# Three chunked recurrences recast from chunks of 64 tokens to blocks of 128

## The chip, the cores and the metric

The kernel runs on one core of one Trainium2 chip. The metric is the device time of one execution in microseconds (us), from the profiler's clock; lower is better. The core has a matrix engine (TensorE, in the profile PE, with its weight loads as PEld), a vector engine (VectorE, DVE), a scalar engine (ScalarE, ACT), GpSimd (POOL) and a queue that issues DMAs (SyncE, SP). The profile also shows the clock that was granted to TensorE as a share of its full level.

## The reference, cut to what matters

Two models of two layers each run one after the other on the same 256 tokens of width 1024. Three recurrences in them are computed chunk by chunk; the reference's chunk is 64 tokens, but each recurrence has the same value for any chunk length.

```python
# 1. HGRN2, in both layers of the first model: 4 heads, dk = dv = 128, log_f per channel
cum = cumsum(log_f)                       # inside a chunk
a   = tril((q*exp(cum-ref)) @ (k*exp(ref-cum)).T)
o   = a @ v + (q*exp(cum)) @ state
state = exp(last)*state + (k*exp(last-cum)).T @ v

# 2. GLA, in the first layer of the second model: 4 heads, dk = 64, dv = 128, the same form,
#    in two directions, over a context of 256 tokens (state only) and then over the 256 tokens

# 3. gated delta rule (GDN), beside GLA: 4 heads, dk = dv = 128, one log decay per token and head
decay = exp(gc_t - gc_s) for s <= t
lmat  = strict_tril((k*beta) @ k.T * decay) + I
u     = lmat^-1 (beta*v - beta*exp(gc)*(k @ state))
o     = exp(gc)*(q @ state) + (q @ k.T * decay) @ u
state = exp(last)*state + (k*exp(last-gc)).T @ u
```

The rest is projections, attention, gated feed-forward layers and, in the last layer, a long convolution through Fourier matrices whose filters are made by a small network.

## The kernel before, in words

Nearly all of TensorE's work are the projections. Each weight is loaded by SP (L470), rounded to a high part by ScalarE (L471), its remainder taken by VectorE (L472), and three products of 128 by 128 weights with 256 tokens are accumulated (L485 to L487, or L521 to L523 where the tokens are the stationary side). A plain float32 product, as the recurrences use, is two instructions in the trace: the 16 calls of L947 are x32 there. The order of instructions on every engine is laid down at build time by a planner that simulates the program; it lets independent work of later lines move forward into waits.

The recurrences stand at these places:

- `br_c_pair` (L892), the HGRN2 of two heads, four times in all (two layers, two pairs). Sums of the log gates inside a chunk (L947, L969), scores by `chunk_scores` (L1081: two products, L1085 and L1087, so that the masked corner is never computed), `masked` (L1090), three state updates (L988 to L995), and the outputs (L1004, L1007).
- `ctx_gla` and `ctx_gdn` run GLA and GDN over the context, next to the feed-forward parts of the first model, so that their small steps lie between projections. `b2_layer0` runs both over the tokens.
- `gla_gates` (L1303) makes the gates and, over the tokens, the scores; `gla_scan` (L1390) walks through four chunks in each direction (L1417, L1419, L1433).
- `gdn` (L1501): gates (L1581 to L1617), decay matrices G (L1619 to L1641), the products with keys and queries (L1657 to L1677), the inverses, and the scan. `block_inverses` (L1461) makes inverses of 16 by 16 blocks on VectorE; L1691 to L1717 double them to 32 and to 64 (L1708 and L1714 on TensorE, a copy between them on ScalarE, a masked copy behind them on VectorE). The scan (L1739 to L1786) takes four chunks in each direction: keys times state (L1749), the right side (L1755), the inverse (L1760), its copy (L1761), the new state (L1765, L1771), queries times state (L1776). L1797 adds the part inside the chunks.

A chunk of 64 tokens takes 64 of the 128 partitions, so its products fill half of the array's rows or columns, or a quarter of the array; in the trace such forms are written 64\*64, 64\*128 or 128\*64 (weight rows by weight columns). In the scans the four heads of a step follow one another in the same half.

`filters` (L2005) makes the filters of the long convolution in eight rounds: loads of a window, a skip row and weights, L2033 and L2044 on TensorE, one addition of the skip row on GpSimd (L2038), and two tiles (fs, fd) written to memory (L2054). It is called for behind the scans of `b2_layer0`, and the planner has moved it into them.

Of the kernel before, what the change touches and what calls it, by code (L numbers as in the profile page):

```python
# [44 lines left out]
def _constants():  # L45
# [17 lines left out]
    add("rev0", same & (i[:, None] > i[None, :]))  # L63
    add("rev1", same & (i[:, None] < i[None, :]))
    j = np.arange(64)
    add("cm0", lo[:, None] <= j[None, :])
    add("cm1", lo[:, None] >= j[None, :])
# [25 lines left out]
def _constants2():  # L93
    f = np.float32
    i = np.arange(128)
    lo = i % 64
    j = np.arange(64)
    parts = []

    def add(name, a):  # L100
        a = np.asarray(a, f).reshape(128, -1)
        o = sum(p.shape[1] for p in parts)
        CST2_COLS[name] = (o, a.shape[1])
        parts.append(a)

    add("neg0", np.where(lo[:, None] <= j[None, :], 0.0, NEG))
    add("neg1", np.where(lo[:, None] >= j[None, :], 0.0, NEG))
# [3 lines left out]
    add("upper", np.stack([i // 32 % 2 == 0, i // 32 % 2 == 1], 1))  # L111
# [139 lines left out]
class K:  # L251
# [640 lines left out]
    def br_c_pair(self, l, p, hh, hl, lp, bh, bl, first):  # L892
# [47 lines left out]

        e1 = lp.tile([128, 2, S], F32, name="ce1")
        e2 = lp.tile([128, 2, S], F32, name="ce2")
        e3 = lp.tile([128, 2, S], F32, name="ce3")
        ps = self.aux()
        for h in range(2):
            for tb in range(2):
                nc.tensor.matmul(ps[:, h * S + tb * 128:h * S + (tb + 1) * 128], lf[:, tb, h * 128:(h + 1) * 128],  # L947
                                 self.c("tri0"), start=True, stop=True)
        v = ps.rearrange("p (c t) -> p c t", t=64)
        ref = lp.tile([128, 8, 1], F32, name="cref")  # L950
# [3 lines left out]
        nc.scalar.activation(e3, ps.rearrange(M2, m=2), AF.Exp)  # L954
        nc.scalar.activation(e2, e1, AF.Exp, scale=-1.0)
        nc.scalar.activation(e1, e1, AF.Exp)
        nc.vector.scalar_tensor_tensor(e1, e1, 0.5, hq, op0=OP.mult, op1=OP.mult)
        dl = lp.tile([128, 2, 4], F32, name="cdl")
        nc.vector.tensor_copy(dl, e3.rearrange("p h (c t) -> p h c t", t=64)[:, :, :, 63])
        nc.vector.scalar_tensor_tensor(e3, e3, 0.5, hq, op0=OP.mult, op1=OP.mult)  # L960
# [5 lines left out]
        nc.vector.tensor_tensor(e2, e2, ps.rearrange(M2, m=2), OP.mult)  # L966
        ps = self.aux()
        for tb in range(2):
            nc.tensor.matmul(ps[:, tb * 256:(tb + 1) * 256], self.c("rev0"), lf[:, tb, :], start=True, stop=True)  # L969
        nc.scalar.activation(e, ps.rearrange(M2, m=2), AF.Exp)  # L970
        nc.vector.tensor_tensor(hk, hk, e, OP.mult)

        AT = lp.tile([128, 4, 64], F32, name="cAT")
        nc.vector.memset(AT, 0.0)
        ps = self.aux()
        for h in range(2):
            for c in range(4):
                u, tb = c % 2, c // 2
                o = (tb * 2 + h) * 64
# [3 lines left out]
        ST = lp.tile([128, 3, 2, 128], F32, name="cST")  # L983
        for c in range(3):
            u, tb = c % 2, c // 2
            ps = self.aux()
            for h in range(2):
                nc.tensor.matmul(ps[:, h * 128:(h + 1) * 128], hk[64 * u:64 * u + 64, tb, h * 128:(h + 1) * 128],  # L988
                                 hv[64 * u:64 * u + 64, tb, h * 128:(h + 1) * 128], start=True, stop=True)
            if c == 0:  # L990
                nc.vector.tensor_copy(ST[:, 0, :, :], ps[:, :256].rearrange("p (h v) -> p h v", h=2))
            else:
                for h in range(2):
                    nc.vector.scalar_tensor_tensor(ST[:, c, h, :], ST[:, c - 1, h, :], dl[:, h, c:c + 1],
                                                   ps[:, h * 128:(h + 1) * 128], op0=OP.mult, op1=OP.add)  # L995
        on = lp.tile([128, 2, 256], F32, tag="cz", name="con")
        ss = lp.tile([128, 4], F32, name="css")
        for tb in range(2):
            po = self.aux()
            for h in range(2):  # L1000
                for u in range(2):
                    c = 2 * tb + u
                    o = po[64 * u:64 * u + 64, h * 128:(h + 1) * 128]
                    nc.tensor.matmul(o, AT[64 * u:64 * u + 64, tb * 2 + h, :],  # L1004
                                     hv[64 * u:64 * u + 64, tb, h * 128:(h + 1) * 128], start=True, stop=(c == 0))
                    if c:
                        nc.tensor.matmul(o, e3[:, h, c * 64:(c + 1) * 64], ST[:, c - 1, h, :], start=False, stop=True)  # L1007
# [73 lines left out]
    def chunk_scores(self, ps, o, u, k, q, d):  # L1081

        nc = self.nc
        full, part = (32, 0) if d == 0 else (0, 32)
        nc.tensor.matmul(ps[64 * u:64 * u + 64, o + full:o + full + 32], k, q[:, full:full + 32], start=True, stop=True)  # L1085
        p = 64 * u + part
        nc.tensor.matmul(ps[p:p + 32, o + part:o + part + 32], k[:, part:part + 32], q[:, part:part + 32], start=True,  # L1087
                         stop=True)

    def masked(self, dst, ps, d):  # L1090

        nc = self.nc
        n = dst.shape[1]
        m = self.c(f"cm{d}").bitcast(U32)
        full, part = (32, 0) if d == 0 else (0, 32)
        nc.vector.copy_predicated(dst[:, :, full:full + 32], m[:, None, full:full + 32].to_broadcast([128, n, 32]),
                                  ps[:, :, full:full + 32])
        for u in range(2):
            r = slice(64 * u + part, 64 * u + part + 32)
            nc.vector.copy_predicated(dst[r, :, part:part + 32], m[r, None, part:part + 32].to_broadcast([32, n, 32]),  # L1100
                                      ps[r, :, part:part + 32])
# [201 lines left out]
    def gla_gates(self, qT, kT, v, lat, smallT, lp, lt):  # L1303
# [16 lines left out]
        q3s, ATs, kds, dls = [], [], [], []  # L1320
        for d in range(2):
# [14 lines left out]
            dl = lp.tile([128, 2, 4], F32, name=f"ldl{d}")  # L1336
            dls.append(dl)
            if lat:
                ps = self.aux()
                for p in range(2):  # L1340
                    for b in range(2):
                        nc.tensor.matmul(ps[:, p * S + b * 128:p * S + (b + 1) * 128],
                                         la[:, b, p * 128:(p + 1) * 128], self.c(f"tri{d}"), start=True, stop=True)
                cv = ps.rearrange(V2, t=64)
                ri = 32 if d == 0 else 31
# [3 lines left out]
                e2 = lt.tile([128, 2, S], F32, tag="le2", name="le2")  # L1349
                e3 = lp.tile([128, 2, S], F32, name=f"le3{d}")  # L1350
                nc.vector.tensor_tensor(e1.rearrange("p a (c t) -> p (a c) t", t=64), cv,
                                        ref.to_broadcast([128, 8, 64]), OP.subtract)
                nc.scalar.activation(e3, ps.rearrange(M2, m=2), AF.Exp, scale=R)
                nc.scalar.activation(e2, e1, AF.Exp, scale=-R)
                nc.scalar.activation(e1, e1, AF.Exp, scale=R)
                nc.vector.tensor_tensor(e1, e1, qT, OP.mult)
                nc.vector.tensor_tensor(e2, e2, kT, OP.mult)
                li = 63 if d == 0 else 0
                nc.vector.tensor_copy(dl, e3.rearrange("p a (c t) -> p a c t", t=64)[:, :, :, li])
                nc.vector.tensor_tensor(e3, e3, qT, OP.mult)  # L1360
                q3s.append(e3)
                AT = lp.tile([128, 8, 64], F32, name=f"lAT{d}")
                nc.vector.memset(AT, 0.0)
                for r in range(2):
                    pa = self.aux()
                    for p in range(2):
                        for c in range(4):
                            u, b = c % 2, c // 2
                            o = (p * 2 + b) * 64
                            self.chunk_scores(pa, o, u, e2[64 * r:64 * r + 64, p, c * 64:(c + 1) * 64],  # L1370
                                              e1[64 * r:64 * r + 64, p, c * 64:(c + 1) * 64], d)
                    self.masked(AT[:, r * 4:r * 4 + 4, :], pa[:, :256].rearrange(V2, t=64), d)
                ATs.append(AT)
            else:
                ps = self.aux()
                for p in range(2):
                    for b in range(2):
                        nc.tensor.matmul(ps[:, p * 4 + b * 2:p * 4 + b * 2 + 2], la[:, b, p * 128:(p + 1) * 128],
                                         self.c("ind64"), start=True, stop=True)
                nc.scalar.activation(dl.rearrange("p a c -> p (a c)"), ps[:, :8], AF.Exp, scale=R)  # L1380
# [865 lines left out]
```

## Time and profile before

| | before |
|---|---|
| time, median of 3 runs | 2060.65 us (2053.74 to 2062.47) |
| the profiled execution | 2056.23 us, span 2054.2 us |
| TensorE busy | 2017.5 us, 98% |
| VectorE, ScalarE, GpSimd busy | 1506.2, 1034.1, 86.1 us |
| mean granted clock of TensorE | 0.982 of full |
| HBM read | 366.27 MB |

Busy time of TensorE counts an instruction from its start to the end of its passage through the array, and instructions overlap there. What an instruction costs the engine is therefore read from the distance between starts: a projection product of 256 columns is 0.28 us long in the timeline, but the next starts 0.12 us later.

### The profile page before, as it was taken

What the parts mean: (1) busy time and instruction counts of PE and PEld (TensorE: products, weight loads), DVE (VectorE), ACT (ScalarE), POOL (GpSimd) and SP (SyncE); (2) the same over time, 40 slices, a digit from 0 to 9 for tenths busy, and PEclk for the clock granted to TensorE, in tenths of its full rate; (3) what the DMA queues carried; (4) which work ended last, traced back from release to release, by engine and by line L of the source; (5) the groups of instructions that cost most, each with busy time, mean ns of one, the idle gap of its engine ahead of it and who ended that gap; (6) DMA issues with size and microseconds to landing.
All of it is one profiled execution on the core that took longest, in us unless ns stands there. A gap on an engine that the chain in (4) does not pass through costs nothing.

```text
span 2054.2 us, 40596 instructions
## 1 busy us (share of the span) xinstructions
PE 2017.5 (98%) x16666; PEld 1918.1 (93%) x16666; DVE 1506.2 (73%) x2491; ACT 1034.1 (50%) x1604; POOL 86.1 (4%) x80
## 2 busy tenths in 40 slices
PE   8999999999999999999999999999989999999998
PEld 8999999999999899999999989897779999899998
DVE  6968877896876868977777855885667555997554
ACT  6553455575544654454655434662135445756443
POOL 0000000010000000000000001000010000001001
PEclk9999999999999999999999999997999999999999
DMA  9854655975567755747654534452215667445664
GB/s 327 274 180 154 222 195 173 320 253 184 188 223 241 236 164 176 244 146 263 203 162 145 175 113 146 161 160 80 68 40 176 195 187 234 156 133 176 194 187 132
DMA packets 118562, 379.36 MB, mean 185 GB/s; under 512 B 18239, under 2 KB 28776, under 8 KB 117096
## 3 DMA queue, kind: packets, MB, share of 16 engines
q1 hardware_dynamic: 118376, 376.76, 56.3%
q8 instruction: 131, 2.15, 0.4%
q14 instruction: 55, 0.45, 0.1%
HBM read 366.27 MB, written 10.25 MB: 183 GB/s over the span
## 4 chain that ended last, share of the span: by engine, by line
PE 92%; DVE 2%; ACT 2%; issue 2%; DMA 1%; POOL 0%; SPq 0%; DVEq 0%; POOLq 0%; ACTq 0%
PE mm L487 22%; PE mm L485 22%; PE mm L486 22%; PE mm L522 1%; PE mm L521 1%; PE mm L523 1%; PE aux L1235 1%; ACT wh L471 1%; DVE wl L472 1%; PE aux L1760 1%; PE aux L1085 1%; PE aux L1765 1%; PE aux L2096 1%; PE mm L2044 1%; PE aux L2079 1%
## 5 line engine op out<-in xcount | busy, mean ns | idle before, releaser
L471 ACT CAST wh<-w 128x1024 fp32r<-128x1024 f32 (+2 forms) x570 | 589.0, 1035 | 665.5 <-PE mm L486 513.1
L472 DVE TENSOR_TENSOR wl<-w,wh 128x1024 fp32r<-128x1024 f32 (+2 forms) x570 | 685.3, 1203 | 290.9 <-ACT wh L471 288.6
L485 PE MATMUL mm<-hh,wh 128*128 128x256 f32 (+1 forms) x1776 | 503.5, 284 | 1.3 <-ACT wh L471 0.7
L487 PE MATMUL mm<-hh,wl 128*128 128x256 f32 (+1 forms) x1776 | 502.0, 283 | 1.1 <-DVE wl L472 1.1
L486 PE MATMUL mm<-hl,wh 128*128 128x256 f32 (+1 forms) x1776 | 502.1, 283 | 0.0
L485 PEld LDWEIGHTS mm<-hh,wh 128*128 128x128 f32 (+1 forms) x1776 | 335.7, 189 | 6.0 <-issue 3.6
L487 PEld LDWEIGHTS mm<-hh,wl 128*128 128x128 f32 (+1 forms) x1776 | 335.7, 189 | 5.1 <-issue 3.0
L486 PEld LDWEIGHTS mm<-hl,wh 128*128 128x128 f32 (+1 forms) x1776 | 335.9, 189 | 3.9 <-issue 2.6
L485 PE MATMUL mm<-xh,wh 128*128 128x256 f32 x960 | 268.7, 281 | 1.0 <-ACT uc L422 0.9
L487 PE MATMUL mm<-xh,wl 128*128 128x256 f32 x960 | 267.5, 279 | 1.6 <-DVE wl L472 1.5
L486 PE MATMUL mm<-xl,wh 128*128 128x256 f32 x960 | 268.3, 281 | 0.2
L487 PE MATMUL mm<-ph,wl 128*128 128x256 f32 x704 | 197.0, 280 | 0.0
L485 PE MATMUL mm<-ph,wh 128*128 128x256 f32 x704 | 196.8, 280 | 0.0
L486 PE MATMUL mm<-pl,wh 128*128 128x256 f32 x704 | 196.6, 279 | 0.0
L487 PEld LDWEIGHTS mm<-xh,wl 128*128 128x128 f32 x960 | 180.3, 188 | 5.2 <-issue 2.5
L485 PEld LDWEIGHTS mm<-xh,wh 128*128 128x128 f32 x960 | 180.4, 188 | 4.1 <-issue 2.2
L486 PEld LDWEIGHTS mm<-xl,wh 128*128 128x128 f32 x960 | 179.8, 188 | 3.8 <-issue 3.0
L1229 DVE SCALAR_TENSOR_TENSOR macc<-mw,cs,macc 128x512 f32<-128x512 f32 x196 | 145.7, 748 | 11.6 <-DMA mw<-in_t_mod_w 10.8
L487 PEld LDWEIGHTS mm<-ph,wl 128*128 128x128 f32 x704 | 132.1, 188 | 1.9 <-issue 1.9
L486 PEld LDWEIGHTS mm<-pl,wh 128*128 128x128 f32 x704 | 132.3, 188 | 1.5 <-issue 1.4
L485 PEld LDWEIGHTS mm<-ph,wh 128*128 128x128 f32 x704 | 132.2, 188 | 1.6 <-issue 1.5
L487 PE MATMUL mm<-brh,wl 128*128 128x256 f32 x384 | 107.5, 281 | 0.0
(679 smaller groups left out, 3595.3 us busy)
## 6 DMA issues: line engine op xcount, KB each, us to landing
w<-in_t_w_in SPq DMA_DIRECT2D x148, 512.0 KB, 4.2
w<-in_t_ffn_w SPq DMA_DIRECT2D x128, 512.0 KB, 4.3
mw<-in_t_mod_w SPq DMA_DIRECT2D x96, 512.0 KB, 4.6
w<-in_t_ffn_w_up SPq DMA_DIRECT2D x88, 512.0 KB, 3.6
w<-in_t_ab_w_in SPq DMA_DIRECT2D x42, 512.0 KB, 4.3
w<-in_t_ffn_w_down SPq DMA_DIRECT2D x40, 512.0 KB, 3.6
w<-in_t_w_lift SPq DMA_DIRECT2D x32, 512.0 KB, 3.8
w<-in_t_hy_w_in SPq DMA_DIRECT2D x24, 512.0 KB, 4.1
```

What stands on the lines that cost most here:

```text
L471: nc.scalar.copy(wh, w)
L472: nc.vector.tensor_tensor(wl, w, wh, OP.subtract)
L485: nc.tensor.matmul(ps, wh, xh, start=start, stop=False)
L486: nc.tensor.matmul(ps, wh, xl, start=False, stop=False)
L487: nc.tensor.matmul(ps, wl, xh, start=False, stop=stop)
L521: nc.tensor.matmul(o, h, wh, start=(k + tb == 0), stop=False)
L522: nc.tensor.matmul(o, h, wl, start=False, stop=False)
L523: nc.tensor.matmul(o, l, wh, start=False, stop=(k == KT - 1 and tb == 1))
L1085: nc.tensor.matmul(ps[64 * u:64 * u + 64, o + full:o + full + 32], k, q[:, full:full + 32], start=True, stop=True)
L1229: nc.vector.scalar_tensor_tensor(acc, v[:, k, :], sc, acc, op0=OP.mult, op1=OP.add)
L1235: nc.tensor.matmul(ps[:, m:m + 1], acc[:, m * 128:(m + 1) * 128], self.ones[:, :1], start=True, stop=True)
L1760: nc.tensor.matmul(ps[r, hs], Y[r, d, h * 2 + b, :], rhs[:, hs], start=True, stop=True)
```

## The change

All three recurrences take blocks of 128 tokens, two in place of four.

- The constants rev, cm and ind64's use in GLA go; `up` (sums over a block), `rest` (sums from behind a token to the block's end) and `mid` (sums counted from the block's middle) come in, and the decay masks neg get 128 columns. `cst` grows by 384 columns, `cst2` by 126.
- Scores: pairs of tokens in the same 64 are still scaled from that chunk's middle token, now by whole 128 by 128 products masked by `tri` (`pairs`); pairs across the two halves get a product of their own, with gates counted from the block's middle (`cross_pairs`). In GLA the keys are kept in two half-zeroed copies (e2w), so that the masked corner stays zero.
- The scans have two steps. In GDN the query product moves ahead of the state update, which is then done in place, and over the tokens only the keys needed (kd) are kept.
- GDN's G and AQ are twice as large, the inverses are doubled once more from 64 to 128 (a product with the off-diagonal part of G and one with the other half's inverse), for which the last doubling also keeps a transposed copy (p3). `block_inverses` gathers and spreads its blocks with four copies of 32 partitions each; X, T and Y are cleared by GpSimd in place of one clearing of T by VectorE; two working tiles share one buffer.
- `filters` uses two buffers fewer: the skip row is loaded into the first row of the sum tile fs, and the difference goes into fe in place of fd.

The core of the diff:

```diff
+    add("up0", i[:, None] <= i[None, :])
+    add("up1", i[:, None] >= i[None, :])
+    add("rest0", i[:, None] > i[None, :])
+    add("rest1", i[:, None] < i[None, :])
...
+    add("mid0", late)
+    add("mid1", late[::-1, ::-1])
...
# br_c_pair
-                self.chunk_scores(ps, o, u, e2[:, h, c * 64:(c + 1) * 64], e1[:, h, c * 64:(c + 1) * 64], 0)
-        self.masked(AT, ps[:, :256].rearrange("p (n t) -> p n t", t=64), 0)
...
+                nc.tensor.matmul(ps[:, g * 128:(g + 1) * 128], e2[:, h, b], e1[:, h, b], start=True, stop=True)
+                nc.tensor.matmul(px[:, g * 64:(g + 1) * 64], f[:, g, :], f[:, g, 64:], start=True, stop=True)
+        self.pairs(AT, ps, 0)
+        self.cross_pairs(AT, px, 0)
...
+    def pairs(self, dst, ps, d):
+        mask = self.c(f"tri{d}").bitcast(U32)[:, None, :].to_broadcast([128, 4, 128])
+        self.nc.vector.copy_predicated(dst, mask, ps.rearrange("p (n t) -> p n t", n=4))
+    def cross_pairs(self, dst, ps, d):
+        r = slice(64 * d, 64 * d + 64)
+        self.nc.scalar.copy(dst[r, :, 64 * (1 - d):64 * (2 - d)], ps[r, :256].rearrange("p (n t) -> p n t", n=4))
...
# gla_gates: scores, one (p, b, r) of sixteen
+                            nc.tensor.matmul(o, e2w[w, d, p, t], e1[w, p, t], start=True, stop=False)
+                            h = slice(32 * (1 - d), 32 * (2 - d))
+                            nc.tensor.matmul(o.rearrange("p (c t) -> p c t", t=64)[:, :, h], e2w[w, 1 - d, p, t],
+                                             e1[w, p, t].rearrange("p (c t) -> p c t", t=64)[:, :, h], start=False,
+                                             stop=True)
...
+                            nc.tensor.matmul(pa[r][:, g * 64:(g + 1) * 64], f[w, g, :], f[w, g, fq], start=True,
+                                             stop=True)
...
# gla_scan and the scan of gdn
-        for n in range(4):
+        for n in range(2):
...
# gdn: behind the doubling to 64
+                        p3 = self.aux()
+                        for n in range(8):
+                            nc.tensor.matmul(p3[us[d], n * 32:(n + 1) * 32], Y[us[d], d, n, us[d]], tv[us[d], n, 0],
+                                             start=True, stop=True)
...
+            p1 = self.aux()
+            for n in range(8):
+                for d in range(2):
+                    nc.tensor.matmul(p1[us[1 - d], n * 64:(n + 1) * 64], gn[d][us[d], n, us[1 - d]], X[us[d], d, n, :],
+                                     start=True, stop=True)
...
+            nc.scalar.copy(W, p1.rearrange("p (n t) -> p n t", n=8))
+            p2 = self.aux()
+            for n in range(8):
+                for d in range(2):
+                    nc.tensor.matmul(p2[us[d], n * 64:(n + 1) * 64], W[us[1 - d], n, :], Y[us[1 - d], d, n, us[1 - d]],
+                                     start=True, stop=True)
+            for d in range(2):
+                nc.vector.tensor_copy(Y[us[d], d, :, us[1 - d]], p2[us[d], :].rearrange("p (n t) -> p n t", n=8))
...
# filters
+                ev, s = (lp.tile(sh, F32, tag=t, name=t) for t in ("fe", "fs"))
+                sk = s[0:1, 0, :]
...
-                        nc.vector.tensor_tensor(d, ev, pv, OP.subtract)
+                        nc.vector.tensor_tensor(ev, ev, pv, OP.subtract)
```

## Rows read from the trace of the kernel before

**Rows 1.** The page: busy time by engine, then the chain that ended last by engine

```profile
PE 2017.5 (98%) x16666; PEld 1918.1 (93%) x16666; DVE 1506.2 (73%) x2491; ACT 1034.1 (50%) x1604; POOL 86.1 (4%) x80
...
PE 92%; DVE 2%; ACT 2%; issue 2%; DMA 1%; POOL 0%; SPq 0%; DVEq 0%; POOLq 0%; ACTq 0%
```

**Rows 2.** Stretches: from:to, length, busy PE, PEld, DVE, ACT, POOL, clock, DMA, GB/s

```profile
70.00:110.00 40.00, 40.00 (x339) 37.28 (x340) 34.42 (x54) 23.03 (x30) 0.00 (x0) 1.00 0.73 238
...
1300.00:1345.00 45.00, 43.79 (x421) 41.08 (x421) 38.58 (x92) 28.89 (x58) 3.28 (x2) 1.00 0.41 133
...
1377.00:1420.00 43.00, 39.70 (x401) 33.23 (x399) 22.99 (x45) 14.17 (x21) 2.35 (x2) 0.68 0.24 72
1420.00:1460.00 40.00, 37.53 (x238) 30.16 (x236) 25.28 (x60) 9.67 (x14) 2.53 (x3) 0.87 0.24 79
```

**Rows 3.** Timeline of PE in one HGRN2 pair: start, length, instruction, shapes, count

```profile
85.55 1.05 PE L947 MATMUL aux<-cst,clf 128*128 128x128 f32 x8
86.44 0.60 PE L964 MATMUL aux<-cst,chk 128*128 128x128 f32 x4
...
96.13 0.30 PE L1085 MATMUL aux<-ce,ce 128*64 128x32 f32 x2
...
99.41 0.72 PE L988 MATMUL aux<-chv,chk 64*128 64x128 f32 x8
100.07 0.38 PE L522 MATMUL mm<-wl,hh 128*128 128x256 f32 x1
...
106.60 0.43 PE L1004 MATMUL aux<-chv,cAT 64*64 64x128 f32 x4
106.96 0.43 PE L1007 MATMUL aux<-cST,ce 128*64 128x128 f32 x2
```

**Rows 4.** Timeline of PE in the token scans of the second model

```profile
1459.15 1.08 PE L1760 MATMUL aux<-drhs,dY 64*64 64x128 f32 x8
1460.17 1.13 PE L2033 MATMUL mm<-fw,hd 128*128 128x256 f32 x4
1461.23 1.16 PE L1765 MATMUL aux<-du,dkd 64*128 64x128 f32 x8
1462.31 1.09 PE L1776 MATMUL aux<-dS,dqT 128*64 128x128 f32 x8
1463.24 1.04 PE L1749 MATMUL aux<-dS,dkT 128*64 128x128 f32 x8
1464.11 0.59 PE L1417 MATMUL aux<-lS,le 128*64 128x256 f32 x2
1464.63 0.65 PE L1419 MATMUL aux<-lv,lAT 64*64 64x128 f32 x4
...
1466.37 1.13 PE L1433 MATMUL aux<-lv,lkd 64*128 64x256 f32 x4
1467.42 1.99 PE L2044 MATMUL mm<-fb,H 128*128 128x256 f32 x8
...
1510.05 5.79 PE L1797 MATMUL aux<-du,dAQ 64*64 64x128 f32 x62
```

**Rows 5.** Timeline of PE: a doubling of the context's inverses, and key products

```profile
1170.37 1.12 PE L1708 MATMUL aux<-dX,dG 64*64 64x32 f32 x32
1171.42 0.39 PE L485 MATMUL mm<-hh,wh 128*128 128x256 f32 x1
...
1334.66 1.10 PE L1673 MATMUL aux<-dkT 128*64 128x64 f32 x32
```

**Rows 6.** Groups of DVE by shape: busy us, mean ns, idle before

```profile
L1755 DVE SCALAR_TENSOR_TENSOR drhs<-aux,dnge,dvtok 64x128 f32<-64x128 f32 x56 | 16.0, 349 | 1.3 <-PE aux L1749 1.2
...
L1634 DVE SCALAR_TENSOR_TENSOR dG<-aux,dgc,cst 128x64 f32<-128x64 f32 x32 | 6.7, 276 | 0.4 <-PE aux L1627 0.3
...
L1677 DVE TENSOR_TENSOR dG<-dG,aux 128x512 f32<-128x512 f32 x4 | 2.5, 678 | 0.0
```

**Rows 7.** DMA issues: size, median us to landing

```profile
spec<-fd SPq DMA_DIRECT2D x8, 256.0 KB, 2.3
```

More of the change, by code (lines that the diff above doesn't have):

```diff
@@ L62, in _constants @@
     add("tri1", same & (i[:, None] >= i[None, :]))
[L63 to L67, printed above, removed]
+    add("up0", i[:, None] <= i[None, :])
+    add("up1", i[:, None] >= i[None, :])
+    add("rest0", i[:, None] > i[None, :])
+    add("rest1", i[:, None] < i[None, :])
+    half = i // 64
+    late = np.where((half[None, :] == 1) & (half[:, None] == 1) & (i[:, None] <= i[None, :]), 1.0, 0.0)
+    late -= np.where((half[None, :] == 0) & (half[:, None] == 0) & (i[:, None] > i[None, :]), 1.0, 0.0)
+    add("mid0", late)
+    add("mid1", late[::-1, ::-1])
     neg = np.zeros((128, 256), f)
@@ L966, in br_c_pair @@
         nc.vector.tensor_tensor(e2, e2, ps.rearrange(M2, m=2), OP.mult)
+        nc.vector.tensor_tensor(f[:, :, :64], f[:, :, :64], ps.rearrange("p (g t) -> p g t", t=128)[:, :, :64], OP.mult)
         ps = self.aux()
[L968 to L973, printed above, removed]
+        nc.tensor.matmul(ps[:, :256], self.c("rest0"), lf[:, 0, :], start=True, stop=True)
@@ L981, in br_c_pair @@
-        self.masked(AT, ps[:, :256].rearrange("p (n t) -> p n t", t=64), 0)
[L983 to L995, printed above, removed]
+            for tb in range(2):
+                g = h * 2 + tb
+                b = slice(tb * 128, (tb + 1) * 128)
+                nc.tensor.matmul(ps[:, g * 128:(g + 1) * 128], e2[:, h, b], e1[:, h, b], start=True, stop=True)
+                nc.tensor.matmul(px[:, g * 64:(g + 1) * 64], f[:, g, :], f[:, g, 64:], start=True, stop=True)
@@ L996, in br_c_pair @@
+        self.pairs(AT, ps, 0)
+        self.cross_pairs(AT, px, 0)
+        ST = lp.tile([128, 2, 128], F32, name="cST")
+        ps = self.aux()
+        for h in range(2):
+            nc.tensor.matmul(ps[:, h * 128:(h + 1) * 128], hk[:, 0, h * 128:(h + 1) * 128],
+                             hv[:, 0, h * 128:(h + 1) * 128], start=True, stop=True)
+        nc.scalar.copy(ST, ps[:, :256].rearrange("p (h v) -> p h v", h=2))
         on = lp.tile([128, 2, 256], F32, tag="cz", name="con")
@@ L1000, in br_c_pair @@
             for h in range(2):
[L1001 to L1007, printed above, removed]
+                o = po[:, h * 128:(h + 1) * 128]
+                nc.tensor.matmul(o, AT[:, h * 2 + tb, :], hv[:, tb, h * 128:(h + 1) * 128], start=True, stop=(tb == 0))
+                if tb:
+                    nc.tensor.matmul(o, e3[:, h, :], ST[:, h, :], start=False, stop=True)
             nc.vector.tensor_copy(on[:, tb, :], po[:, :256])
@@ L1363, in gla_gates @@
                 nc.vector.memset(AT, 0.0)
-                for r in range(2):
[L1365 to L1372, printed above, removed]
+                pa = [self.aux() for _ in range(2)]
@@ new lines, in gla_gates @@
+                for r in range(2):
+                    self.pairs(AT[:, r * 4:r * 4 + 4, :], pa[r], d)
+                pa = [self.aux() for _ in range(2)]
+                for p in range(2):
+                    for b in range(2):
+                        for r in range(2):
+                            g, w = p * 2 + b, slice(64 * r, 64 * r + 64)
+                            nc.tensor.matmul(pa[r][:, g * 64:(g + 1) * 64], f[w, g, :], f[w, g, fq], start=True,
+                                             stop=True)
@@ L1373, in gla_gates @@
+                for r in range(2):
+                    self.cross_pairs(AT[:, r * 4:r * 4 + 4, :], pa[r], d)
                 ATs.append(AT)
@@ L1496, in block_inverses @@
             turn(B, C)
-            dv = dst.rearrange("p d n (i e t) -> p i t (d n) e", i=2, e=2)
-            nc.scalar.activation(dv[:, 0], B, AF.Copy, scale=up[:, 0:1])
-            nc.vector.tensor_scalar(dv[:, 1], B, up[:, 1:2], None, op0=OP.mult)
+            n = dst.shape[3] // 32
+            dv = dst.rearrange("p d n (i e t) -> p i t (d n) e", i=n, e=2)
+            for i in range(4):
+                r = slice(32 * i, 32 * i + 32)
+                (nc.vector.tensor_copy if i % 2 else nc.scalar.copy)(dv[r, i % n], B[r])
     def gdn(self, xh, xl, lat, gab, lp, states, side=None, vp=None, first=()):
@@ L1684, in gdn @@
             T = ip.tile([128, 2, 8, 64], F32, name="dT")
-            nc.vector.memset(T, 0.0)
+            for t in (X, T, Y):
+                nc.gpsimd.memset(t, 0.0)
+            gn = [G[:, d].rearrange("p h b t -> p (h b) t") for d in range(2)]
+            us = [slice(64 * u, 64 * u + 64) for u in range(2)]
             def half(t, d, bs, h):
```

369 lines of the change are left out of this document (179 added, 190 removed).

## The prediction

> **What bounds the kernel now.** The page comes first: TensorE is busy for 98% of the span, and the chain that ended last consists of TensorE for 92% [rows 1]. So a microsecond taken from TensorE's queue is a microsecond of the span, as long as nothing else becomes late. Busy time can't say what an instruction costs that queue, because instructions overlap in the array; I take the distance from one start to the next in the timeline. Eight full-array instructions of 128 columns (L947) start at 85.55 and the next line at 86.44: 0.111 us each [rows 3]. Four of 256 columns (L2033) take 1460.17 to 1461.23, 0.265 with the change of form; I use 0.25 [rows 4].
>
> The windows then say where TensorE has company. In the first HGRN2 VectorE is busy 34.4 of 40 us, in the token GDN's preparation 38.6 of 45, at full clock. From 1377 on there are few projections left, and the granted clock is 0.68 over 43 us and 0.87 over the next 40 [rows 2]. The clock has two levels, 1.2 and 2.4 GHz, so 0.68 means 64% of that window at the lower one: 27.5 us, and 10.4 in the next.
>
> Now the recurrences' own prices. A GDN step's four heads (8 instructions) cost 1.02 us at the inverse (L1760), 1.08 at the state (L1765), 0.93 (L1776) and 0.87 (L1749), although they fill half the array or a quarter; a full-array group would be 8 x 0.111 = 0.89. A GLA pair costs 0.52 to 0.58 (L1417), 0.58 (L1419), 1.05 (L1433) [rows 4]. So the cost goes by instructions, and half as many steps halve it. Only where neighbouring instructions lie in different halves are small forms cheap: 32 of L1708 in 1.05 us, and 32 of L1673 within 1.10, 33 ns each [rows 5].
>
> Here a rule speaks against the change. The Trainium skill, TensorEngine Tiling, Tiling Modes, says that tiles of a divided array load weights and multiply independently, in parallel. If the scans ran two at a time so, their 57 us below would be 28 and GDN would gain 4 in place of 32, some 2033 us in all; rows 4 show one group behind another at 127 ns an instruction, rows 5 the parallel case, and I go by them.
>
> **The change part by part** (counts from the code, two instructions to a product).
>
> *GDN scans.* Before: 14 groups L1749 x 0.87 = 12.2, 16 L1760 x 1.02 = 16.3, 14 L1765 x 1.08 = 15.1, 8 L1776 x 0.93 = 7.4, L1797 5.8 [rows 4]: 56.8. After: 10 groups for the context, 14 for the tokens, 4 for AQ: 28 x 0.89 = 24.9. **-31.9.** VectorE's L1755 and its like are halved too: 128 rows take what 64 take, 349 ns [rows 6].
>
> *HGRN2, per pair.* Scores 96.13 to 99.41 = 3.28; L988 0.66 and once more about 0.64; output 12 places of 0.36; sums L969 about 0.67 [rows 3]: 9.6. After: 4 score products 0.89; 4 cross products of 64 columns, between half of that and all of it, 0.8 taken since the weight load stays; sums 0.44 more for `up` and 0.4 for `rest`; state 0.44; output 6 products 1.33: 4.3. Four pairs: **-21.2** (bounds -19 to -23).
>
> *GLA scans.* Before 16 x 0.55 + 16 x 0.58 + 14 x 1.05 = 32.8; after 16 x 0.25 + 32 x 0.111 + 24 x 0.25 = 13.6: **-19.2.** The context's decays by one column fewer products: **-0.8.**
>
> *GLA scores.* Before 32 calls at HGRN2's 0.41 = 13.1. After 96 instructions with 64 weight rows: 32 of 128 columns, 64 of 64 columns. Bounds: 33 ns (L1673) gives 3.2, 135 ns (L1765, always the same half) gives 13. The halves alternate only every four instructions, so I take 0.098, 9.4; the second sum (`up` beside `mid`) adds 1.8. **-1.9** (bounds -8 to +2).
>
> *GDN preparation, both passes.* Narrow sums in place of L1615's about +0.2; L1627's 32 small instructions (about 2.0) become 16 of 256 columns, 4.0, twice: +4.0; the key and query products lose their cheap form, 1.05 to 1.78, three times: +2.1. **+6.3.**
>
> *Inverses, per pass.* p3's 32 instructions all lie in one quarter: between 33 ns and L1760's 127, I take 115, 3.7. The two products of the last doubling alternate between quarters: 64 instructions, 33 to 60 ns, 3.0 taken. Twice: **+13.4** (bounds 6 to 16).
>
> Sum on TensorE: -55.3.
>
> *What isn't TensorE's.* The scan's groups stand among projections, and the first instruction behind a change of form takes about 0.1 us more (L522 at 100.07 is 0.38 long, the projections' usual is 0.28) [rows 3]; some 80 groups fewer, half of them at such a border: -4. VectorE's preparation of GDN grows: 16 of L1634 from 276 to about 349 ns, and 12 more operations between L1634's and L1677's size, about 5 us in a stretch where it is busy 86% [rows 2, 6]; hidden for the context by feed-forward work, 3 us shown for the tokens. The inverse chain gains a level (about 2 + 0.6 + 2 + 1.4 us and hand-overs) and about 4 us from the four-copy gathering and the shared buffer. For the context projections cover it; for the tokens the filters' TensorE work does. If that cover is gone it costs 11; I take 4. `cst` and `cst2` are 0.26 MB longer in a start that loads at capacity: 1. GpSimd's clearing (no row; between VectorE's rate, a few us, and 16 us at its own additions' rate) lies beside VectorE's work on the blocks of 16, some 40 us: 0. ScalarE gets about 1 us more per HGRN2 pair, at half load [rows 1, 2]: 0. Waits in all: +8.
>
> Total -55.3 - 4 + 8 = -51. The profiled execution took 2056.2 us, which gives 2005; the median of the runs is 0.2% above it. **I predict 2005 us.**
>
> **The rivals.**
>
> *A, the token stretch gains nothing.* Of the sum some 25 us fall between 1377 and 1510. If the chain of inverses and scans, not TensorE, ends last there, they are lost: **2028**. The filters could do it: each round now loads the skip row into fs, so SP holds that load, and the weights queued behind it, until the last round's fs has reached memory (2.3 us landing [rows 7]); then the load, GpSimd, L2044, a copy, L2044 and two operations: about 10 us a round, 80 for eight, against some 108 us of TensorE work left there (133 less 25). It decides once a round passes 13.5 us. Nothing waits for the filters until the last layer, so projections may pass them; against that, every queue is in order.
>
> *B, VectorE is the bound at HGRN2.* At 86% [rows 2] it may not follow a TensorE that is through an eighth sooner; the 21 us shrink to nothing: **2026**. Against it: it loses the state operations and half of three others there, some 1.6 us a pair.
>
> *C, the clock (the slower side).* If the token stretch with less small work ran wholly at 1.2 GHz, the time would grow: its 108 us hold 38 at the lower level today, so they are 89 us of work at full clock, 178 at the lower one, 70 more than I count: -51 becomes +19, **2075**. It turns the sign once three quarters of what runs at full clock there falls to the lower level. For it: the level falls in just this stretch [rows 2]. Against: it falls where 64\*64 forms of 32 columns run, and these give way to full-array products. The Trainium skill, TensorE: Matmul & The Clock Gate, Part 1, says that the lower level is the default which activity lifts; by it fewer gaps would mean the upper level, and these rows agree so far.
>
> *D, the clock never falls there:* the 38 us at the lower level cost 19 less, and 6 of the 8 us of waits go: **1980**.
>
> **How the numbers follow.** My forecast with its own range of 1988 to 2018 holds 0.64, A 0.15, B 0.07, D 0.08, C 0.03, and a gain eaten by several waits so that no change is measured 0.03. The likeliest is 2005; reaching to D below and A above gives 1978 to 2032, which leaves out C and little else. About 0.5% is what a measurement of this kernel can tell from no change, so faster means below 2050: 0.93, same 0.03, slower 0.04.
>
> **What would show it.** L1760's line at 64 instructions in place of 128, at 128\*128 and about 0.111 us from start to start; HGRN2's scores through in about 1.7 us in place of 3.28; the distance from GDN's first doubling to the last output product of the tokens some 25 us shorter; VectorE near 90% in GDN's preparation. I am wrong if the groups of the scans stand apart with waits for VectorE or ScalarE between them (A), if L2044 waits for GpSimd in every round (A), if the clock row of that stretch lies below 0.65 (C), or if full-array products next to one another cost more than 0.13 us.

## The result, and the profile after

The changed kernel takes 2007.14 us, the median of four runs (2005.55 to 2007.61), against 2061.56 us for the kernel before on the same chip: a ratio of 0.9735, 95% interval 0.9699 to 0.9771. The predicted 2005 us lies 2 us from it. As the rows will show, that nearness is partly luck: two large misses cancelled.

The page of the changed kernel, busy time and then the chain that ended last (answers [rows 1]):

```profile
PE 1950.2 (97%) x16274; PEld 1889.9 (94%) x16274; DVE 1487.3 (74%) x2374; ACT 1049.6 (52%) x1640; POOL 96.4 (5%) x86
...
PE 88%; DVE 4%; ACT 3%; issue 2%; DMA 2%; POOL 0%; SPq 0%; DVEq 0%; POOLq 0%; ACTq 0%
```

TensorE is busy 67 us less, but the span, now 2003.8 us, is only 50 us shorter: the engine's idle time grew from 37 us (2054.2 less 2017.5) to 54. The profiled execution itself took 2005.55 us.

To see where, both executions are cut at the same places: the root of the mean squares on GpSimd at each layer's norms. First the kernel before, then the kernel after (start, length, instruction):

```profile
434.16 0.71 POOL L334 TENSOR_TENSOR rsq<-ms,cst 128x2 f32<-128x2 f32 x1 [9.27 <-DVE ms L373]
659.54 0.71 POOL L334 TENSOR_TENSOR rsq<-ms,cst 128x2 f32<-128x2 f32 x1 [17.64 <-DVE ms L373]
1027.62 0.71 POOL L334 TENSOR_TENSOR rsq<-ms,cst 128x2 f32<-128x2 f32 x1 [8.47 <-DVE ms L373]
1285.67 0.71 POOL L334 TENSOR_TENSOR rsq<-ms,cst 128x2 f32<-128x2 f32 x1 [19.90 <-DVE ms L373]
1554.91 0.71 POOL L334 TENSOR_TENSOR rsq<-ms,cst 128x2 f32<-128x2 f32 x1 [7.68 <-DVE ms L373]
```

```profile
423.77 0.89 POOL L337 TENSOR_TENSOR rsq<-ms,cst 128x2 f32<-128x2 f32 x1 [10.14 <-DVE ms L376]
643.77 0.71 POOL L337 TENSOR_TENSOR rsq<-ms,cst 128x2 f32<-128x2 f32 x1 [17.64 <-DVE ms L376]
992.66 0.71 POOL L337 TENSOR_TENSOR rsq<-ms,cst 128x2 f32<-128x2 f32 x1 [7.41 <-DVE ms L376]
1268.29 0.71 POOL L337 TENSOR_TENSOR rsq<-ms,cst 128x2 f32<-128x2 f32 x1 [5.36 <-DVE ms L376]
1502.41 0.71 POOL L337 TENSOR_TENSOR rsq<-ms,cst 128x2 f32<-128x2 f32 x1 [6.02 <-DVE ms L376]
```

| stage between these rows | before | after | difference |
|---|---|---|---|
| start, first layer with HGRN2 | 434.2 | 423.8 | -10.4 |
| feed-forward with the context's GLA | 225.4 | 220.0 | -5.4 |
| second layer with HGRN2 | 368.1 | 348.9 | -19.2 |
| feed-forward with the context's delta rule | 258.1 | 275.6 | **+17.6** |
| GDN and GLA over the tokens | 269.2 | 234.1 | **-35.1** |
| the rest | 499.3 | 501.4 | +2.1 |

Four stages shrink; the one with the context's delta rule grows.

**What went as priced.** HGRN2 of the first pair (answers [rows 3]):

```profile
100.72 0.49 PE L995 MATMUL aux<-ce,ce 128*128 128x128 f32 x2 [0.19 <-DVE ce L969]
101.05 0.33 PE L996 MATMUL aux<-cf 128*128 128x64 f32 x2
...
102.56 0.66 PE L1003 MATMUL aux<-chv,chk 128*128 128x128 f32 x4
```

From the first score product at 100.72 to the state product at 102.56 pass 1.84 us, where the chunks took 3.28 and 1.7 were forecast. The token scans (answers [rows 4]):

```profile
1432.43 1.06 PE L1791 MATMUL aux<-dS,dkT 128*128 128x128 f32 x8
1433.33 1.06 PE L1800 MATMUL aux<-dS,dqT 128*128 128x128 f32 x8
...
1465.07 0.60 PE L1443 MATMUL aux<-lS,le 128*128 128x256 f32 x2
1465.50 0.61 PE L1445 MATMUL aux<-lv,lAT 128*128 128x128 f32 x4
```

A group of four heads takes 0.90 us from L1791 to L1800 (0.89 forecast), one GLA product of 256 columns, which is two instructions, 0.43 (0.50 forecast): about what full-array products were taken at.

**What did not.** TensorE in the context's delta rule, after:

```profile
1015.93 0.28 PE L490 MATMUL mm<-hh,wl 128*128 128x256 f32 x1
1019.49 0.36 PE L488 MATMUL aux<-cxh,wh 128*128 128x256 f32 x1 [3.28 <-DVE dkT L1268]
...
1041.07 0.60 PE L1566 MATMUL aux<-cst,dvT 128*128 128x128 f32 x4
...
1051.51 2.07 PE L1643 MATMUL aux<-drows,cst 8*128 8x256 f32 x4
1053.52 0.58 PE L488 MATMUL mm<-hh,wh 128*128 128x256 f32 x1
```

Between 1015.93 and 1053.52 no feed-forward projection (mm<-hh) runs at all; TensorE has only the context's own work, which waits for VectorE and for its weights. In the windows (from:to, length, busy PE, PEld, DVE, ACT, POOL, clock, DMA, GB/s) it is idle for 12.3 us and its clock falls:

```profile
1015.00:1035.00 20.00, 13.40 (x80) 12.18 (x79) 10.25 (x20) 7.43 (x23) 1.64 (x1) 0.83 0.33 106
1035.00:1055.00 20.00, 14.34 (x74) 11.38 (x73) 10.12 (x19) 7.60 (x10) 1.84 (x2) 0.75 0.00 1
1055.00:1075.00 20.00, 20.00 (x88) 17.40 (x88) 11.66 (x29) 4.28 (x6) 0.00 (x0) 0.57 0.09 27
```

Why the projections stop is seen on VectorE:

```profile
1046.55 1.29 DVE L1567 TENSOR_TENSOR dvtok<-aux,dik 128x512 f32<-128x512 f32 x2 [0.78 <-PE aux L1566]
1047.76 0.40 DVE L1614 COPY drows<-aux 8x256 f32<-8x256 f32 x1
1048.09 1.86 DVE L558 TENSOR_TENSOR f<-mm,pb 128x512 f32<-128x512 f32 x3
```

L558 takes a finished feed-forward product out of PSUM, and three stand in its queue at once, right behind the context's last value tiles: all three PSUM tiles of the projections had been full. In the built program the reason can be read from the tiles' places. Y and G of the context grew by 4 KB a partition each and lie above the context's copies cxh and cxl, which thereby moved down; the longer constants moved the feed-forward tiles up by 1.5 KB. cxh now starts at byte 151,360 of a partition, and the feed-forward gate tiles (f2) end at 154,560. Before, it was 160,064 against 153,024. A pool's new tile waits for the old one on its bytes, so f2 can't be written before the last value projection (to 1041.07) has read cxh. Only f2 shares bytes. That the copy into f1 stands late as well, and that all three come 7 us after 1041.07, behind the value tiles, is the planner's order, which nothing here explains.

### The profile page after: what moved, and what is told of

Same layout as the page of the kernel before. It is cut to its first block, busy times and chain, and to the rows that moved or that the text cites. A ratio compares the mean times of both kernels' runs of the same rounds, so it can differ in the third digit from the quotient of the medians.

```text
span 2003.8 us, 39753 instructions
## 1 busy us (share of the span) xinstructions
PE 1950.2 (97%) x16274; PEld 1889.9 (94%) x16274; DVE 1487.3 (74%) x2374; ACT 1049.6 (52%) x1640; POOL 96.4 (5%) x86
## 4 chain that ended last, share of the span: by engine, by line
PE 88%; DVE 4%; ACT 3%; issue 2%; DMA 2%; POOL 0%; SPq 0%; DVEq 0%; POOLq 0%; ACTq 0%
PE mm L490 23%; PE mm L488 23%; PE mm L489 23%; DVE wl L475 2%; ACT wh L474 1%; PE aux L1230 1%; PE mm L524 1%; PE mm L525 1%; PE mm L526 1%; PE mm L2080 1%; PE aux L2132 1%; PE aux L490 1%; PE aux L2115 1%; PE aux L861 1%; PE aux L488 1%
## 5 line engine op out<-in xcount | busy, mean ns | idle before, releaser
L488 PE MATMUL mm<-hh,wh 128*128 128x256 f32 x1776 | 502.7, 283 | 2.3 <-ACT bq L768 2.0
L489 PE MATMUL mm<-hl,wh 128*128 128x256 f32 x1776 | 501.2, 282 | 0.0
L488 PEld LDWEIGHTS mm<-hh,wh 128*128 128x128 f32 x1776 | 335.2, 189 | 6.1 <-ACT bq L768 2.4
L489 PEld LDWEIGHTS mm<-hl,wh 128*128 128x128 f32 x1776 | 335.1, 189 | 3.0 <-issue 2.3
L488 PE MATMUL mm<-brh,wh 128*128 128x256 f32 x384 | 107.8, 281 | 0.0
```

The costliest lines, as they stand in the source:

```text
L488: nc.tensor.matmul(ps, wh, xh, start=start, stop=False)
L489: nc.tensor.matmul(ps, wh, xl, start=False, stop=False)
```

## The experiments

Each ratio is against runs of the kernel before on the same chip.

**1. The memory edit.** On the changed kernel, G's pool is opened behind the context's convolutions:

```diff
-        b1 = es1.enter_context(self.pool("db1", side))
+        if lat:
+            b1 = es1.enter_context(self.pool("db1", side))
...
                 r2 = keys()
                 values()
+            b1 = es1.enter_context(self.pool("db1", side))
```

> The changed kernel with one edit of memory: for the context, the pool of the decay matrices G is opened behind the convolutions of keys and values, not ahead of them. No instruction is added or removed; the two copies of the context (cxh, cxl) come to lie 8 KB higher and share no bytes any more with the gate tiles (f2) of the feed-forward part beside them. Theory, shared memory: in the changed kernel the feed-forward evictions could not write f2 before the last value projection had read cxh, so its PSUM tiles stayed full, TensorE ran dry for some 12 us between 1016 and 1048 us and worked at the lower clock behind that. Without the sharing the stage from the norm at 992.7 to the norm at 1268.3 us takes 256 to 260 us in place of 275.6, and the time is 1986 to 1992 us. Rival, longer chain: the context's preparation is dearer by blocks of 128, and TensorE waits for that chain itself; then the stage stays within 3 us of 275.6 and the time at 2003 to 2009 us.

Measured: 0.965 (0.9607 to 0.9693), some 17 us less than the changed kernel's 0.9735. The context's stage in its profile:

```profile
993.52 0.71 POOL L337 TENSOR_TENSOR rsq<-ms,cst 128x2 f32<-128x2 f32 x1 [7.41 <-DVE ms L376]
1246.71 0.71 POOL L337 TENSOR_TENSOR rsq<-ms,cst 128x2 f32<-128x2 f32 x1 [5.36 <-DVE ms L376]
```

```profile
1015.00:1035.00 20.00, 20.00 (x172) 20.00 (x171) 14.93 (x25) 11.45 (x28) 1.64 (x1) 1.00 0.56 186
1035.00:1055.00 20.00, 20.00 (x172) 20.00 (x171) 15.08 (x21) 10.20 (x15) 1.91 (x2) 1.00 0.33 106
1055.00:1075.00 20.00, 20.00 (x132) 17.58 (x130) 11.42 (x22) 7.39 (x10) 0.00 (x0) 0.85 0.40 132
```

It takes 253.2 us in place of 275.6 (256 to 260 expected), and the gaps are gone. The longer-chain rival falls: the same chain no longer leaves TensorE idle. Behind the stage, from the norm at 1246.71 to the one at 1676.52, the profiled execution took 430 us where the changed kernel took 418 (1268.29 to 1686.66); so the time gains less than the stage. TensorE's waits hardly differ there: new ones for VectorE (3.6 us at L1343, 3.3 at L1886) stand against others that went, 17.2 us in place of 15.2. Six of the 11 us lie behind the tokens (190.6 us in place of 184.3), where the same instructions run in both with 0.8 us of waits, at a granted clock of 1.00: there the projections start 118 ns apart in place of 113. Nothing here shows why. The clock still falls from 1055 us on (0.85, and 0.81 in the next 20 us): that is another cause, tested in run 8.

**2. The same overlap in the kernel before.** An unused tile, and not one instruction changed:

```diff
         b1 = es1.enter_context(self.pool("db1", side))
+        if not lat:
+            b1.tile([128, 2560], F32, name="dpad")
```

> The kernel before with an unused tile of 10 KB a partition ahead of the context's copies, so that they share with the feed-forward part's f2 the same bytes as in the changed kernel. Not one instruction of the computation differs. Shared memory: the stage from the norm at 1027.6 to the norm at 1285.7 us (258.1 long) grows by 12 to 25 us, and the time by as much, 2070 to 2083 us. Rival, longer chain: blocks of 64 leave the chain as short as it was, and the time stays at 2054 to 2065 us.

Measured: 1.0136 (1.01 to 1.0173), 28 us slower; the stage in its profile:

```profile
1036.00 0.71 POOL L334 TENSOR_TENSOR rsq<-ms,cst 128x2 f32<-128x2 f32 x1 [8.47 <-DVE ms L373]
1324.17 0.71 POOL L334 TENSOR_TENSOR rsq<-ms,cst 128x2 f32<-128x2 f32 x1 [18.61 <-DVE ms L373]
```

288.2 us in place of 258.1, more than the 12 to 25 expected. cxh then starts at 149,824, below f2's end at 153,024: the same 3,200 shared bytes as in the changed kernel. Both directions together show it: the bytes that two pools share cost the changed kernel what it lost there.

**3. The filters' skip rows.** On the memory edit, the rows go into the Fourier matrices' tiles, which are empty at that time:

```diff
-                sk = s[0:1, 0, :]
+                sk = (self.Fm if q < 2 else self.Gm.rearrange("p k n -> p (k n)"))[0:1, q % 2 * 256:q % 2 * 256 + 256]
```

> The memory edit of the run before, and beside it the filters' skip rows loaded into the Fourier matrices' tiles, which are empty until the filters are through, in place of the first row of the sum tile: no round's load waits any more until the last round's sum has reached memory. In the changed kernel the rounds stand about 12 us apart, each addition on GpSimd waits for its load, and TensorE waits 3.1 us for them and 2.5 us for the state of GLA, whose load stands behind the filters' in SP's queue. If the filters' rounds set a part of the token stretch (the prediction's rival A), this is 4 to 12 us faster than the memory edit alone; if TensorE's queue sets it, at most 4 us faster, and the rounds merely move.

Measured: 0.964 (0.9598 to 0.9682), not to be told from the memory edit's 0.965. In the changed kernel GpSimd's addition waits for its load in seven of eight rounds, as rival A had it:

```profile
1411.25 0.74 POOL L2075 TENSOR_TENSOR fb<-fb,fs 1x256 f32<-1x256 f32 x1 [17.57 <-DMA fs<-in_hy_skip]
1424.56 0.72 POOL L2075 TENSOR_TENSOR fb<-fb,fs 1x256 f32<-1x256 f32 x1 [12.57 <-DMA fs<-in_hy_skip]
```

Without that wait the rounds still stand 12.6 us apart on average (12.2 in the changed kernel). With intervals of some 9 us each the times can't tell a gain of a few us from none; in the profiles the stage of the tokens takes 236.4 us in place of run 1's 239.2. So the wait was real and cost some 3 us by these two traces, far from the 25 of rival A.

**4. Blocks of 64, directions alternating.** The kernel before; in the delta rule's scan each group of products runs over both directions, whose chunks always lie in opposite halves:

```diff
-                    for h in range(4):
-                        nc.tensor.matmul(ps[r, h * 128:(h + 1) * 128], kT[:, h, c * 64:(c + 1) * 64], src[:, h, :],
-                                         start=True, stop=True)
+                for h in range(4):
+                    for d in range(2):
+                        nc.tensor.matmul(ps[rs[d], h * 128:(h + 1) * 128], kT[:, h, cs[d] * 64:(cs[d] + 1) * 64],
+                                         sds[d][0][:, h, :], start=True, stop=True)
```

and likewise for the other three groups.

> The kernel before, blocks of 64, with the instructions of the delta rule's scan in another order: the two directions of a step, which always lie in opposite halves of the array, alternate head by head. The same products, the same shapes, the same counts. Theory, price by instruction: a product of 64 rows or 64 columns costs its 110 to 135 ns whatever stands beside it; the time stays within 6 us of the kernel before, and may grow by the waits of two directions in lock step. Rival, halves in parallel: at 32 columns alternating neighbours cost 33 ns, so at 128 columns about 65 in place of 127; the 52 groups of the scans with 51 us shrink to 26 to 30, and the time is 2030 to 2042 us, which would be most of what the change gained in the delta rule's scans.

Measured: 0.9914 (0.9889 to 0.9939), 18 us faster (13 to 23): outside the theory's 6, at the lower edge of the rival's 20 to 32. The timeline of its token scan:

```profile
1451.13 1.09 PE L1784 MATMUL aux<-dS,dqT 128*64 128x128 f32 x16
1452.15 1.13 PE L2054 MATMUL mm<-fb,H 128*128 128x256 f32 x4
...
1463.39 1.09 PE L1763 MATMUL aux<-drhs,dY 64*64 64x128 f32 x16
1464.41 1.13 PE L1433 MATMUL aux<-lv,lkd 64*128 64x256 f32 x4
```

Sixteen instructions take 1.02 us (1451.13 to 1452.15, and 1463.39 to 1464.41), 64 ns each: the theory of a price by instruction falls, and the rival's price holds for the forms 64\*64 and 128\*64. Whole groups of the form 64\*128 (L1770) cost between 69 and 103 ns an instruction. Added up from start to start, the scan's four lines shrink from 56.4 to 36.7 us; not by half, also because in places the groups were torn apart by other work or one direction came alone (eight of L1770 in 1.08 us from 1447.90).

**5 to 7. One recurrence at a time.** The kernel before with the changed code of one recurrence and its constants.

> The kernel before with HGRN2 alone by blocks of 128 (its three new constants added); GLA and the delta rule stay at 64. Theory, TensorE's queue by instruction: the prediction's term of 21.2 us, with the granted clock of the two stretches behind HGRN2 coming back to 1.00 as in the changed kernel (some 8 us more): 18 to 30 us faster than before. Rival, VectorE binds there (the prediction's B): less than 8 us faster.

HGRN2 alone: 0.9892 (0.9845 to 0.994), 22 us faster. VectorE doesn't bind it.

> The kernel before with GLA alone by blocks of 128, context and tokens. By TensorE's queue: scans 19 us less, scores and decays 3 to 8 less, second sum 2 more; 19 to 26 us faster than before, nearly all of it between 1340 and 1520 us. Rival, the token stretch is bound by the delta rule's chain and the filters beside it (the prediction's A): 0 to 8 us faster, since GLA's work there is cover and not path.

GLA alone: 0.9882 (0.9851 to 0.9913), 24 us. In its profile the stage of the tokens takes 247.6 us in place of 269.2: GLA's work there is on the path.

> The kernel before with the delta rule alone by blocks of 128, with the G pool opened behind the context's convolutions, so that no memory is shared with the feed-forward part. By TensorE's queue: scans 32 to 36 less, preparation 6 (as predicted) to 17 (as its lines in the changed kernel add up, partly at the lower clock) more, inverses 8 more: 6 to 20 us faster than before. Rival, price of small forms wrong altogether: no gain, or slower by up to 10. With the two runs beside it this tells whether the three parts add up: the sum of the three gains against the 70 us or so that the changed kernel gained with its memory edit.

The delta rule alone, with the memory edit: 0.9923 (0.9895 to 0.9951), 16 us. The three gains make 62 us, against 72 of the changed kernel with the memory edit; with intervals of 6 to 10 us each they may simply add up.

**8. Full weight rows in the preparation.** On run 3:

```diff
-        rows = b2.tile([8, 2, S], F32, name="drows")
+        rows = b2.tile([128, 2, S], F32, name="drows")
+        nc.gpsimd.memset(rows, 0.0)
...
-        return self.ident[:8, r:r + 1].to_broadcast([8, n])
+        return self.ident[:, r:r + 1].to_broadcast([128, n])
```

> The kernel of the own skip rows, with one edit in the delta rule's preparation: the eight rows of log decays (drows) lie in a tile of 128 partitions of which the rest is zero, so that the products that spread them over G use 128 weight rows in place of 8. The same count of instructions and columns. In the runs so far the granted clock falls to 0.5 just where these products stand without projections between them, in the context's and in the tokens' preparation, some 14 us at the lower level each. Theory, a nearly empty array lowers the clock: it stays at 1.00 there, 6 to 14 us faster than the own skip rows. Rival, the gaps and few columns of the whole stretch lower it: the clock row is as before, and the time within 3 us.

Measured: 0.9572 (0.9547 to 0.9597), 14 us less than run 3 by the ratios. Windows of run 3, then of this one, first in the context's preparation, and as the last row in that of the tokens:

```profile
1060.00:1070.00 10.00, 10.00 (x66) 8.84 (x64) 4.20 (x8) 3.10 (x4) 0.00 (x0) 0.86 0.42 147
1070.00:1080.00 10.00, 10.00 (x33) 7.85 (x34) 5.69 (x18) 2.42 (x4) 0.00 (x0) 0.50 0.16 54
1080.00:1090.00 10.00, 10.00 (x52) 9.16 (x52) 6.28 (x12) 2.00 (x2) 0.00 (x0) 0.62 0.13 39
...
1275.00:1300.00 25.00, 22.54 (x104) 19.50 (x104) 16.45 (x47) 11.03 (x31) 1.64 (x1) 0.64 0.24 83
```

```profile
1060.00:1070.00 10.00, 10.00 (x77) 9.22 (x76) 5.29 (x11) 4.10 (x5) 0.00 (x0) 1.00 0.45 157
1070.00:1080.00 10.00, 10.00 (x79) 9.71 (x78) 9.77 (x26) 4.25 (x5) 0.00 (x0) 1.00 0.16 55
1080.00:1090.00 10.00, 10.00 (x87) 10.00 (x86) 9.50 (x14) 7.61 (x8) 0.00 (x0) 1.00 0.46 158
...
1265.00:1290.00 25.00, 22.54 (x146) 20.59 (x146) 20.02 (x53) 15.14 (x39) 1.64 (x1) 0.86 0.30 102
```

In the context, the same products over zeros in 120 more rows leave the clock at its upper level, and the three windows hold 243 instructions in place of 151. In the tokens' preparation the level still falls, for some 7 us of 25 in place of 18 (0.86 and 0.64), and in run 3 it falls some 10 us before these products, behind waits and among sums of 8 columns; so weight rows are a cause there, but not the only one. The two stages take 247.1 and 227.5 us, where run 3 took 256.4 and 236.4. Four of the products themselves last 2.07 us in run 3 (L1645 at 1075.97, 8\*128) and 1.02 here (L1646 at 1072.51, 128\*128).

**9. Sums of both blocks at once, scores alternating.** On run 8, `up`, `rest` and the sums of a block take 16 columns in place of twice 8, and GLA's first two score products go round both halves before the next pair:

```diff
-                for a, m in enumerate((f"up{d}", f"rest{d}")):
-                    o = ((a * 2 + b) * 2 + d) * 8
-                    nc.tensor.matmul(pt[:, o:o + 8], self.c(m), g[:, b, :], start=True, stop=True)
+            for a, m in enumerate((f"up{d}", f"rest{d}")):
+                o = (a * 2 + d) * 16
+                nc.tensor.matmul(pt[:, o:o + 16], self.c(m), g.rearrange("p b j -> p (b j)"), start=True, stop=True)
```

> The kernel of the full rows with two orders of TensorE changed. The sums of the delta rule's preparation take both blocks at once, 16 columns in place of twice 8, so 10 of 20 small instructions go in each of the two passes; each cost about 140 ns at full clock, so 2.8 us. GLA's scores alternate between the two halves of the weight rows at every product in place of every second one; 64 instructions cost 80 to 93 ns each, and if halves in parallel bring them to about 55, 2 us. Both: 2 to 6 us faster than the full rows, 0.952 to 0.957 of the kernel before. Rival, this work stands beside waits of VectorE: within 1 us, 0.957.

Measured: 0.9498 (0.9477 to 0.9519), 1965.38 us against run 8's 1971.59: 6 us less by the medians, at the upper end of what was expected. From start to start the sums take 2.3 us in place of 5.4, the first two score products 4.4 in place of 6.4: 5 of the 6 us. The ratios lie further apart, since the kernel before took 2068.89 us on this run's chip and 2062.75 on the other; the two were not run side by side. It beats the kernel before by 5% and the changed kernel by 2%.

## Why the prediction was right, and where it was not

*The bound.* TensorE's queue sets the time: each part's removal of small products brought about its sum in the time, also over the tokens. Right.

*GDN scans, -31.9.* Full-array groups cost 0.89 to 0.90 us as taken; the lines of the scan add up to 26 us from start to start (24.9 forecast). Right for the new form; the old one was priced too low, since the kernel before's lines add up to 62.5 us without a wait of 3.8 at L1797 (56.8 forecast), in part at the lower clock.

*HGRN2, -21.2.* 22 us alone. Right. In the changed kernel the two layers lost 10.4 and 19.2; part of the second's surplus is the clock, which before stood at 0.90 over 750 to 800 us and after at 1.00; the rest stays open.

*GLA, -19.2 - 0.8 - 1.9.* 24 us alone against 22. The scans' lines add up to 13.8 us after (13.6 forecast), the scores' to 7.9 (9.4). Right in sum, not in each term: before, the scans' lines add up to 30.6 (32.8 forecast) and the scores' to 16.0 (13.1), and the context's decays take 1.7 us in both kernels, since their 16 instructions only lost a column.

*Inverses, +13.4.* Over-sized: p3's 32 instructions in one quarter cost 56 ns each (thirteen from 1399.44 to 1400.17), where 115 was taken, and the last doubling 36 ns. Both passes together add 8 us.

```profile
1399.44 0.94 PE L1730 MATMUL aux<-dT,dY 64*64 64x32 f32 x13
1400.17 0.24 PE L1735 MATMUL aux<-dY,dT 64*64 64x32 f32 x1
...
1402.01 1.14 PE L1747 MATMUL aux<-dX,dG 64*64 64x64 f32 x30
1403.08 0.66 PE L1398 MATMUL aux<-lf 64*128 64x64 f32 x4
```

*GDN preparation, +6.3.* Under-sized. From start to start its lines grew by 17: sums +4.7 in place of +0.2 (an instruction of 8 columns still costs about 0.14 us), L1643 +9 in place of +4, the key and query products +3.7 in place of +2.1. The count of columns was right, but not the clock that the new form gets: 8 weight rows with 256 columns, 32 times, and the level falls to 0.50 around them. At the upper level they cost the 0.25 us taken. Run 8 shows the weight rows as the cause of most of it: the 32 take 7.4 us there, 13.3 in the changed kernel.

*Waits, +8.* Wrong in place and size. The prediction sought them on VectorE, in the chain of inverses and at the start; the largest lay in none of these. It counted the work of each edit and not the bytes: a tile that grows moves its neighbours, and a pool's tile waits for whoever holds its bytes. That is the +17.6 stage: 12.3 us of gaps and some 34 us at the lower level there; run 1 made the stage 22 us shorter.

*Over the tokens, -25.* The stage became 35 us shorter. Over the four windows of 50 us from 1350 the kernel before spent 47 us at the lower level (0.88, 0.81, 0.94, 0.90); the changed kernel over four from 1300 spent 27 (0.86, 0.93, 0.97, 0.97): 10 us, part of rival D.

So the total was right because two misses largely cancelled: the context's delta rule, for which the terms give about -5, came out at +17.6, while the tokens came out 10 and the second layer 9 better than forecast.

*The rule against the change.* The prediction went by the rows of neighbours in one half and priced a scan group at 127 ns an instruction, and said that only alternating halves are cheap. Run 4 shows both: alternating neighbours cost 64 ns at 128 columns. The Trainium skill, TensorEngine Tiling, Tiling Modes, says that tiles work independently; this trace agrees once neighbours lie in different tiles. What the prediction did not see is that the kernel before could have had about half of the scans' gain by an order alone (18 us, 13 to 23 by the interval, of 31.9).

*The rivals.* A falls: the stage of the tokens gained 35 us, and taking away its wait brought some 3 more (its price should read 2030, which is 2005 and the 25 lost). B falls by run 5. C falls, though the reason given against it holds only in part: GLA's forms of 32 columns went, the inverses' did not (576 instructions in place of 512). D holds in part.

*What was to show it.* The inverse's line (L1812) stands at 64 full-array instructions, 0.104 us from start to start on average, and the HGRN2 scores are through in 1.84 us: right. VectorE near 90% in GDN's preparation was wrong: 34.8 of 45 us (77%), beside a clock of 0.85. In run 8, with the clock at 0.92 over the same work, it is 39.0 (87%), so the lower clock is part of it:

```profile
1300.00:1345.00 45.00, 44.32 (x305) 42.11 (x306) 34.79 (x75) 21.43 (x30) 5.94 (x4) 0.85 0.26 82
...
1271.00:1316.00 45.00, 44.40 (x340) 43.22 (x341) 39.04 (x83) 23.32 (x32) 5.12 (x4) 0.92 0.31 106
```

The distance from the tokens' first doubling to GDN's last output product shrank by 58 us, not 25 (131.5 to 73.2): the planner moved GLA's scan (11 us) and filter products (10 us) behind that product, so it measured the order and not the work. To the last output product of both, GLA's at 1469.00, it shrank by 36, like the stage. It was a poor sign to choose. Of the signs of being wrong none came: TensorE waited for GpSimd in two of the eight filter rounds, and no clock row of the stretch lay below 0.65.

## What to carry to other kernels

Price a change on a full engine by the distance between starts, per shape, and ask of each small shape which half of the array its neighbours use: an order that alternates halves may give most of what a larger block gives. When a tile grows, look up what it pushes down and whose bytes it then shares; a wait for memory shows in no count of instructions, and an edit that only moves a pool can prove it from both sides. A sum that comes out right should still be checked stage by stage against the trace.

## What the runs showed of the hardware that was not expected

- Groups of 128 columns whose neighbours lie in opposite halves cost 64 ns an instruction at 64\*64 and 128\*64 (69 to 103 at 64\*128); in one half they cost 109 to 135. 32 columns in one quarter cost 56.
- Products with 8 weight rows stood where the granted clock fell to 0.50; in the context the same products with 120 rows of zeros beside them ran at 1.00, in the tokens' preparation the level still fell, for some 7 us in place of 18. The whole kernel became 14 us faster by that edit alone.
- The same projections, without waits and at a granted clock of 1.00, start 113 ns apart in one profile and 118 in another. Behind the tokens the stage takes 184.3 or 190.6 us by that (changed kernel and run 1): a third of what one recurrence gained.
